# Sparse attention scores two heads at a time, block 0 with two products for three; the first weights by ScalarE's queue

## Chip, cores and metric

The kernel runs on one core of a Trainium2 chip. The metric is the device time of one execution in microseconds; a figure for a kernel is the median of its runs.

## What is computed

A decoder trunk of two layers on 512 tokens of width 2048, all in 32-bit floats. Layer one is sparse attention: an indexer picks 128 keys for each query, and 16 heads with 4 shared key/value heads attend to them. Layer two is stick-breaking attention. Each layer ends with a residual, a layer norm and a gated embedding. The part that the change touches most:

```python
proj = x @ w_in
q, k, v, gate, iq, ik, iw = jnp.split(proj, SPLITS_A, axis=-1)
...
# per block of 128 queries: n_sel = 128 keys, chosen by the indexer's scores
logits = jnp.einsum('bqngd,bqknd->bqngk', qg, ksel) * (HEAD_DIM ** -0.5)
logits = jnp.where(valid, logits, -jnp.inf)
wts = jax.nn.softmax(logits, axis=-1)
o = jnp.einsum('bqngk,bqknd->bqngd', wts, vsel)
...
return (o * jax.nn.silu(gate)) @ w_o
```

## The kernel before

Every product of 32-bit operands is done as three products of split operands. `split` writes the rounded part (`wh`, `xh`, `qh`, ...) with ScalarE and the rest (`wl`, `xl`, `ql`, ...) with VectorE; `mm3` (lines 136 to 138) multiplies high by high, low by high and high by low into one PSUM bank.

Weights come in tiles `raw` of 128x2x512, three in turn, issued by SP (`next_raw`, line 201 for the first pieces, 203 for the rest). `weight_parts` has three pairs `wh`, `wl` in turn. TensorE works in the order of the program text (`manual_schedule`); the order of VectorE, ScalarE and GpSimd is made by the framework's scheduler when the kernel is built, and each of these engines then works strictly in that order.

The start: VectorE writes a zero tile by a memset and a copy, TensorE runs six products of zeros (`spun`, line 158), and `first_items` splits the first pieces of x and of the weights of the indexer's queries (`iq`) and the keys (`k`).

The sparse attention runs over four groups g of four heads. `attend(g, Q)` is a generator: `scores(i)` for the query blocks i = 0 to 3 (block i has 128 (i + 1) keys), and `apply(i)`, which transposes the softmax tile (`pt`), splits it (`ph` by ScalarE, `pl` by VectorE) and multiplies by the values (`o`). Each head's score is an `mm3` into a bank `s`; VectorE adds the mask `am[i]` and takes the maximum in one custom instruction (reduction), a small step scales the maximum, ScalarE does exp with the sum, VectorE takes the reciprocal and scales. Score and transpose banks come from `spare`, which gives three banks in turn.

`interleave` puts steps of the gate projection (`gemm_w`, tiles `g`; one step is one `mm3`, 512 wide) between the yields of `attend`: first `lead` steps, then an even share of `n_fill` over `n_main` yields, and the rest at the end. `merge` takes in turn one step of `scores(i + 1)` and one of `apply(i)`. The place of the yields so sets how much other work TensorE has between one head's score and the next.

```python
yield from scores(0)
for i in range(4):
    following = scores(i + 1) if i < 3 else iter(())
    if i == 0:
        for _ in range(2):
            next(following)
            yield
    yield from merge(following, apply(i))
```

Of the kernel before, what the change touches and what calls it, by code (L numbers as in the profile page):

```python
# [10 lines left out]
F32 = mybir.dt.float32  # L11
F32R = mybir.dt.float32r
I32 = mybir.dt.int32
AF = mybir.ActivationFunctionType
ALU = mybir.AluOpType
# [3 lines left out]
T = 512  # L19
H = T // 2  # L20
# [36 lines left out]
def interleave(main, n_main, fill, n_fill, lead=0):  # L57

    steps(fill, lead)
    done = 0  # L60
    for i, _ in enumerate(main, 1):
        steps(fill, n_fill * i // n_main - done)
        done = n_fill * i // n_main
    run(fill)
# [13 lines left out]
def trunk_kernel(  # L78
# [56 lines left out]
    def mm3(out, a, b, start, stop):  # L135
        pe.matmul(out, a[0], b[0], start=start, stop=False)  # L136
        pe.matmul(out, a[0], b[1], start=False, stop=False)  # L137
        pe.matmul(out, a[1], b[0], start=False, stop=stop)  # L138
# [11 lines left out]
    def fblock(n):  # L150
        return F[n // 4][:, n % 4]

    zeros = XL[15][:, :128]
    dve.memset(fblock(0)[:, :128], 0.0)
    dve.tensor_copy(zeros, fblock(0)[:, :128])
    spun = bank(7, "spun")
    for _ in range(6):
        pe.matmul(spun.rearrange("p (a n) -> p a n", a=4), zeros, zeros.unsqueeze(1).broadcast_to([128, 4, 128]), start=True, stop=True)

    def plain(kb):  # L160
        return XH[kb], XL[kb]
# [17 lines left out]
    def next_raw():  # L179
        while sent[0] < len(units) and len(raws) < 3:  # L180
            raw = top.tile([128, 2, 512], F32, name="raw", tag="raw", bufs=3)
            unit = units[sent[0]]
            if len(unit) == 1:
                _, k, n = unit[0].shape
            else:
                k, n = 2, unit[-1]
            raw = raw.rearrange("p a n -> p (a n)")[:, : k * n].rearrange("p (k n) -> p k n", k=k)
            if len(unit) == 1:
                nc.sync.dma_start(raw, unit[0])
            else:  # L190
                src, a, b, c0, n = unit
                rows = src.rearrange("(k p) n -> p k n", p=128)
                step = b - a
                if sent[0] < 2:

                    for i, cut in enumerate(((0, H if sent[0] else NSEL, T), (0, T))):
                        for lo, hi in zip(cut, cut[1:]):
                            halves.append((raw[:, i, lo:hi], rows[:, a + i * step, c0 + lo : c0 + hi]))
                    if len(halves) == 6:
                        for n in (1, 3, 4, 2, 5, 0):  # L200
                            nc.sync.dma_start(*halves[n])
                else:
                    nc.sync.dma_start(raw, rows[:, a : b + 1 : step, c0 : c0 + n])
            raws.append(raw)
            sent[0] += 1
        return raws.popleft()
# [43 lines left out]
    def first_items():  # L250

        for k2 in range(NK // 2):
            x = next_raw()
            for n in (2 * k2, 2 * k2 + 1) if k2 else ():

                was, pinned[0] = pinned[0], k2 > 1
                split(*plain(n), x[:, n % 2])
                pinned[0] = was
            if k2 == 2:
                tc.keep_in_program_order(nc.sync.dma_start(rc, rope_c))  # L260
            if k2 in (2, 3):
                half = slice(64 * (k2 - 2), 64 * (k2 - 1))
                tc.keep_in_program_order(nc.sync.dma_start(posi[half], pos.broadcast_to([64, T])))
            if k2 == NK // 2 - 1:
                tc.keep_in_program_order(nc.sync.dma_start(lnc, ln_c))
            for c in range(2):
                raw = next_raw()
                if k2 == 0 and c:
                    split(*(part[:, :NSEL] for part in plain(0)), x[:, 0, :NSEL])
                for a in range(2):  # L270
                    wh, wl = weight_parts()
                    if k2 == c == 0:
                        cuts = ((NSEL, T), (0, H), (H, T)) if a == 0 else ((0, T),) * 2
                        for n, (lo, hi) in enumerate(cuts):
                            parts, src = (plain(a), x) if n == 0 else ((wh, wl), raw)
                            hp, lp = (part[:, lo:hi] for part in parts)
                            if n == 0:
                                dve.tensor_copy(hp, src[:, a, lo:hi])
                            else:
                                act.activation(hp, src[:, a, lo:hi], AF.Copy)  # L280
                            dve.tensor_tensor(lp, src[:, a, lo:hi], hp.bitcast(F32), ALU.subtract)
                    else:
                        split(wh, wl, raw[:, a])
                    yield wh, wl
# [4 lines left out]
    def gemm_w(items, get, banks, n=512, order=range(NK)):  # L289

        for i, kb in enumerate(order):
            wh, wl = next(items)
            x = get(kb)
            for j, out in enumerate(banks):
                a, b = j * 128, min(n, (j + 1) * 128)
                mm3(out[: b - a], (wh[:, a:b], wl[:, a:b]), x, i == 0, i == len(order) - 1)
                yield
# [442 lines left out]
    pi_.close()  # L740
    pkv_ = ExitStack()
    pkv = pkv_.enter_context(ss(name="pkv", bufs=1, side="right"))
    K = [tuple(pkv.tile([128, T], F32R, name=f"k{s}{g}") for s in "hl") for g in range(4)]
    V = [tuple(pkv.tile([128, 512], F32R, name=f"v{s}{t}") for s in "hl") for t in range(4)]

    def split_queries(g):
# [69 lines left out]
    def attend(g, Q):  # L816
        d = slice(g * 128, (g + 1) * 128)
        P = {}

        def scores(i):  # L820
            w = 128 * (i + 1)
            s = slice(i * 128, w)
            sm = pb.tile([128, 4, 4], F32, name="sm", tag="sm", bufs=2)
            P[i] = pb.tile([128, 4, 384 + 128 * (i % 2)], F32, name="p", tag=f"p{i % 2}")
            for h in range(4):
                ps = spare("s")
                mm3(ps[:, :w], [q[:, s] for q in Q[h]], [k[:, :w] for k in K[g]], True, True)
                p = P[i][:, h, :w]
                mx, nm, rs, ri = (sm[:, h, j : j + 1] for j in range(4))
                dve.tensor_tensor_reduce(p, ps[:, :w], am[i], 1.0, GONE, ALU.add, ALU.max, mx)  # L830
                dve.tensor_scalar(nm, mx, -HSCALE, None, ALU.mult)
                act.activation(p, p, AF.Exp, bias=nm, scale=HSCALE, accum_out=rs)
                dve.reciprocal(ri, rs)
                dve.tensor_scalar(p, p, ri, None, ALU.mult)
                yield

        def apply(i):
            po = bank(7, "o")
            ready = []

            def values(kb, parts):
                mm3(po, [v[:, d] for v in V[kb]], parts, kb == 0, kb == i)

            for kb in range(i + 1):
                pt = spare("pt")
                for h in range(4):
                    pe.transpose(pt[:, h * 128 : (h + 1) * 128], P[i][:, h, kb * 128 : (kb + 1) * 128], ident)
                parts = tuple(pb.tile([128, 512], F32R, name=f"p{x}", tag=f"p{x}", bufs=2) for x in "hl")
                split(*parts, pt)
                yield  # L850
                if ready:
                    values(*ready.pop())
                    yield
                ready.append((kb, parts))
            values(*ready.pop())
            act.activation(F[g][:, :, i * 128 : (i + 1) * 128], po.rearrange("p (h q) -> p h q", h=4), AF.Copy)
            yield

        yield from scores(0)
        for i in range(4):  # L860
            following = scores(i + 1) if i < 3 else iter(())
            if i == 0:
                for _ in range(2):
                    next(following)
                    yield
            yield from merge(following, apply(i))

    for g in range(4):
        banks = mm_banks("g")
        interleave(attend(g, Q), 36, gemm_w(items, plain, banks), 50 - 6 * (g == 0), lead=8 + 6 * (g == 0))  # L870
        if g < 3:
            Q = split_queries(g + 1)
        for h in range(4):
            sg = pb.tile([128, T], F32, name="sg", tag="sg", bufs=3)
            act.activation(sg, banks[h], AF.Silu)
            dve.tensor_tensor(F[g][:, h], F[g][:, h], sg, ALU.mult)
# [513 lines left out]
```

## Time and profile before

| | |
|---|---|
| median of 3 runs | 1872.39 us |
| lowest, highest | 1872.07, 1872.66 us |
| profiled execution | 1871.96 us |
| its span | 1870.2 us |
| TensorE busy | 1863.4 us (100%) |
| VectorE, ScalarE busy | 1196.2 (64%), 940.9 us (50%) |
| first scores of g = 0, 1, 2, 3 start at | 371.97, 431.11, 494.40, 557.66 us |
| in 372 to 608 us: VectorE, ScalarE busy | 147.44, 127.64 of 236.00 us |

The table's engine times are the sum of what each engine was busy with; busy shares say little by themselves where an engine waits in one stage and is pressed in another. PE is TensorE, DVE VectorE, ACT ScalarE; a line number is one of the kernel's, and line 111 is the helper through which all VectorE and ScalarE instructions go. A row of the timeline gives start, duration, engine, line, operation, output and inputs, shape, and in brackets the idle time of the engine before it and what ended that.

### The profile page before, as it was taken

The numbers are of one execution on the slowest core, as the hardware profiler recorded it, in microseconds if no ns is written. First come the engines' busy times: TensorE is split into PE (matmuls) and PEld (weight loads), VectorE is DVE, ScalarE is ACT, GpSimd is POOL, SyncE is SP. The second block draws the span as 40 slices with busy tenths as digits, with TensorE's granted clock in tenths as the row PEclk, the third lists the DMA queues.
The fourth block names the chain that finished last, engine by engine and source line by source line (L and its number), as shares of the span: only waits on it lengthen the run. The fifth ranks groups of instructions, "written<-read, shape, count | busy, mean of one in ns | idle before, by whom it ended". The sixth has DMA issues, their size and how long they took to land.

```text
span 1870.2 us, 24902 instructions
## 1 busy us (share of the span) xinstructions
PE 1863.4 (100%) x9229; PEld 1586.1 (85%) x9229; DVE 1196.2 (64%) x2326; ACT 940.9 (50%) x1712; POOL 26.8 (1%) x46
## 2 busy tenths in 40 slices
PE   9999999999999999999999999999999999999998
PEld 8898888888888888888888999988888888888887
DVE  5668678566556444675467788877656645567534
ACT  3546333355554432474245444478877743347422
POOL 0000000000000000000000000000100000000000
PEclk9999999999999999999999999999999999999999
DMA  6442333322222532333334333323222253243333
GB/s 197 127 121 61 102 90 102 91 67 68 68 69 59 162 117 79 124 101 102 124 124 124 102 102 102 108 85 90 59 68 69 64 183 100 74 130 94 120 102 113
DMA packets 111178, 189.21 MB, mean 101 GB/s; under 512 B 8528, under 2 KB 29008, under 8 KB 111056
## 3 DMA queue, kind: packets, MB, share of 16 engines
q1 hardware_dynamic: 111056, 187.62, 33.1%
q8 instruction: 72, 1.18, 0.3%
q14 instruction: 50, 0.41, 0.1%
HBM read 179.21 MB, written 8.39 MB: 100 GB/s over the span
## 4 chain that ended last, share of the span: by engine, by line
PE 99%; ACT 0%; DVE 0%; issue 0%; ACTq 0%
PE g L136 12%; PE g L138 12%; PE g L137 12%; PE o L137 7%; PE o L138 7%; PE o L136 7%; PE m L136 4%; PE m L138 4%; PE m L137 4%; PE q L137 3%; PE q L136 3%; PE q L138 3%; PE k L137 2%; PE k L138 2%; PE k L136 2%; PE z L1272 2%
## 5 line engine op out<-in xcount | busy, mean ns | idle before, releaser
L111 ACT ACTIVATE wh<-raw 128x512 fp32r<-128x512 f32 (+3 forms) x685 | 397.9, 582 | 702.0 <-PE g L137 234.1
L111 DVE TENSOR_TENSOR wl<-raw,wh 128x512 fp32r<-128x512 f32 (+3 forms) x685 | 430.9, 630 | 473.7 <-ACT wh L111 458.3
L136 PE MATMUL g<-xh,wh 128*128 128x512 f32 x1024 | 403.7, 394 | 0.1
L138 PE MATMUL g<-xh,wl 128*128 128x512 f32 x1024 | 399.4, 390 | 0.0
L137 PE MATMUL g<-xl,wh 128*128 128x512 f32 x1024 | 399.4, 390 | 0.0
L138 PEld LDWEIGHTS g<-xh,wl 128*128 128x128 f32 x1024 | 192.2, 188 | 40.8
L136 PEld LDWEIGHTS g<-xh,wh 128*128 128x128 f32 x1024 | 192.4, 188 | 38.3 <-ACT wk L111 0.8
L137 PEld LDWEIGHTS g<-xl,wh 128*128 128x128 f32 x1024 | 192.5, 188 | 37.0
L138 PE MATMUL o<-xh,wl 128*128 128x512 f32 x512 | 199.3, 389 | 0.0
L137 PE MATMUL o<-xl,wh 128*128 128x512 f32 x512 | 199.2, 389 | 0.0
L136 PE MATMUL o<-xh,wh 128*128 128x512 f32 x512 | 199.2, 389 | 0.0
L138 PEld LDWEIGHTS o<-xh,wl 128*128 128x128 f32 x512 | 96.1, 188 | 20.2 <-DVE wl L111 0.3
L137 PEld LDWEIGHTS o<-xl,wh 128*128 128x128 f32 x512 | 96.1, 188 | 20.1
L136 PEld LDWEIGHTS o<-xh,wh 128*128 128x128 f32 x512 | 96.1, 188 | 19.9
L136 PE MATMUL q<-xh,wh 128*128 128x512 f32 x256 | 99.6, 389 | 0.0
L137 PE MATMUL q<-xl,wh 128*128 128x512 f32 x256 | 99.6, 389 | 0.0
L138 PE MATMUL q<-xh,wl 128*128 128x512 f32 x256 | 99.6, 389 | 0.0
L111 ACT ACTIVATE sh<-st 128x512 fp32r<-128x512 f32 x80 | 49.7, 624 | 44.4 <-DVE st L111 44.3
L111 DVE TENSOR_TENSOR sl<-st,sh 128x512 fp32r<-128x512 f32 x80 | 55.2, 691 | 13.9 <-ACT sh L111 13.9
L111 DVE TENSOR_TENSOR xl<-f,xh 128x512 fp32r<-128x512 f32 x80 | 54.3, 686 | 12.6 <-ACT f L111 12.3
L111 ACT ACTIVATE wk<-z 128x512 f32<-128x512 f32 x80 | 47.2, 590 | 23.8 <-PE z L138 16.3
L136 PEld LDWEIGHTS q<-xh,wh 128*128 128x128 f32 x256 | 48.0, 188 | 10.1
(289 smaller groups left out, 3340.1 us busy)
## 6 DMA issues: line engine op xcount, KB each, us to landing
raw<-w_in_a SPq DMA_DIRECT2D x95, 512.0 KB, 3.7
raw<-w_in_b SPq DMA_DIRECT2D x64, 512.0 KB, 3.8
raw<-w_ple_gate SPq DMA_DIRECT2D x52, 512.0 KB, 3.7
raw<-w_o_a SPq DMA_DIRECT2D x24, 512.0 KB, 3.8
raw<-w_o_b SPq DMA_DIRECT2D x24, 512.0 KB, 3.7
raw<-w_kv_b SPq DMA_DIRECT2D x16, 512.0 KB, 3.7
raw<-w_ple_gate SPq DMA_DIRECT2D x24, 256.0 KB, 2.9
f<-xT SPq DMA_DIRECT2D x4, 1024.0 KB, 6.5
```

Source lines behind the costliest of these rows:

```text
L111: ins = method(*args, **kw)
L136: pe.matmul(out, a[0], b[0], start=start, stop=False)
L137: pe.matmul(out, a[0], b[1], start=False, stop=False)
L138: pe.matmul(out, a[1], b[0], start=False, stop=stop)
L1272: pe.matmul(z, m, p, start=False, stop=n == len(terms), skip_group_check=True)
```

## The change

The keys of a group are now one tile with the high and low parts side by side. For block 0 (128 keys) one product multiplies the high queries by both parts, 256 columns into the two halves of the bank, and a second one adds low queries by high keys onto the first half; a new VectorE instruction adds the mask to the second half, and the reduction takes that in place of the mask. For blocks 0 to 2, `scores` yields after every second head; block 3 yields after each. `attend` has 30 yields in place of 36, and one step of `scores(1)`, which is two heads, goes ahead of the merge in place of two steps of one head.

At the start the zero tile is one memset, the sixth warm-up product is half as wide, the first piece of weights is issued by ScalarE in place of SP, and its first half is split in two pieces of 128 columns, with the order of ScalarE and VectorE fixed for these.

```diff
-    dve.memset(fblock(0)[:, :128], 0.0)
-    dve.tensor_copy(zeros, fblock(0)[:, :128])
+    dve.memset(zeros.bitcast(F32), 0.0)
     spun = bank(7, "spun")
-    for _ in range(6):
-        pe.matmul(spun.rearrange("p (a n) -> p a n", a=4), zeros, zeros.unsqueeze(1).broadcast_to([128, 4, 128]), start=True, stop=True)
+    for n in (4, 4, 4, 4, 4, 2):
+        out = spun.rearrange("p (a n) -> p a n", a=4)[:, :n]
+        pe.matmul(out, zeros, zeros.unsqueeze(1).broadcast_to([128, n, 128]), start=True, stop=True)
...
                     if len(halves) == 6:
-                        for n in (1, 3, 4, 2, 5, 0):
+                        nc.scalar.dma_start(*halves[3])
+                        for n in (1, 4, 2, 5, 0):
                             nc.sync.dma_start(*halves[n])
...
                     if k2 == c == 0:
-                        cuts = ((NSEL, T), (0, H), (H, T)) if a == 0 else ((0, T),) * 2
+                        pinned[0] = a == 0
+                        cuts = ((NSEL, T), (0, 128), (128, H), (H, T)) if a == 0 else ((0, T),) * 2
...
+                        pinned[0] = False
...
-    K = [tuple(pkv.tile([128, T], F32R, name=f"k{s}{g}") for s in "hl") for g in range(4)]
+    KT = [pkv.tile([128, 2, T], F32R, name=f"k{g}") for g in range(4)]
+    K = [(kt[:, 0], kt[:, 1]) for kt in KT]
...
             for h in range(4):
                 ps = spare("s")
-                mm3(ps[:, :w], [q[:, s] for q in Q[h]], [k[:, :w] for k in K[g]], True, True)
                 p = P[i][:, h, :w]
                 mx, nm, rs, ri = (sm[:, h, j : j + 1] for j in range(4))
-                dve.tensor_tensor_reduce(p, ps[:, :w], am[i], 1.0, GONE, ALU.add, ALU.max, mx)
+                mask = am[i]
+                if i:
+                    mm3(ps[:, :w], [q[:, s] for q in Q[h]], [k[:, :w] for k in K[g]], True, True)
+                else:
+                    qh, ql = (q[:, s] for q in Q[h])
+                    two = ps[:, : 2 * w].rearrange("p (a k) -> p a k", a=2)
+                    pe.matmul(two, qh, KT[g][:, :, :w], start=True, stop=True)
+                    pe.matmul(ps[:, :w], ql, K[g][0][:, :w], start=False, stop=True, skip_group_check=True)
+                    mask = pb.tile([128, 128], F32, name="s1", tag="s1", bufs=2)
+                    dve.tensor_tensor(mask, two[:, 1], am[i], ALU.add)
+                dve.tensor_tensor_reduce(p, ps[:, :w], mask, 1.0, GONE, ALU.add, ALU.max, mx)
                 dve.tensor_scalar(nm, mx, -HSCALE, None, ALU.mult)
                 act.activation(p, p, AF.Exp, bias=nm, scale=HSCALE, accum_out=rs)
                 dve.reciprocal(ri, rs)
                 dve.tensor_scalar(p, p, ri, None, ALU.mult)
-                yield
+                if i == 3 or h % 2:
+                    yield
...
             if i == 0:
-                for _ in range(2):
-                    next(following)
-                    yield
+                next(following)
+                yield
             yield from merge(following, apply(i))
...
-        interleave(attend(g, Q), 36, gemm_w(items, plain, banks), 50 - 6 * (g == 0), lead=8 + 6 * (g == 0))
+        interleave(attend(g, Q), 30, gemm_w(items, plain, banks), 50 - 6 * (g == 0), lead=8 + 6 * (g == 0))
```

## The prediction

> **What bounds the kernel now.** I read the page first, then the waits of TensorE, then the timeline around the edited places.
>
> ```profile
> span 1870.2 us, 24902 instructions
> PE 1863.4 (100%) x9229; PEld 1586.1 (85%) x9229; DVE 1196.2 (64%) x2326; ACT 940.9 (50%) x1712; POOL 26.8 (1%) x46
> PE 99%; ACT 0%; DVE 0%; issue 0%; ACTq 0%
> PE spun L158 <- DVE xl L111: 1.4, 1, 1.4
> PE z L1272 <- DVE sl L111: 0.2, 1, 0.2
> ```
>
> TensorE is busy for all of the span, the chain that ended last is 99% TensorE, and the last two lines (waiter, releaser, us, times, longest) say that it waits for nobody after its start. So only two things move the end: TensorE getting fewer or shorter instructions, and TensorE being made to wait where it does not wait now. The order in which the build puts the instructions is the same before and after except in the first microseconds and in the four attention groups (372 to 608 us); nothing else has to be priced.
>
> **Part 1, fewer score products: a gain.** The timeline of TensorE at the first score of g = 1 and at a 256-wide one (start, duration, instruction):
>
> ```profile
> 430.65 0.39 PE L137 MATMUL g<-xl,wh 128*128 128x512 f32 x1
> 430.88 0.39 PE L138 MATMUL g<-xh,wl 128*128 128x512 f32 x1
> 431.11 0.22 PE L136 MATMUL s<-kh,qh 128*128 128x128 f32 x1
> 431.28 0.27 PE L138 MATMUL s<-kh,ql 128*128 128x128 f32 x1
> 431.67 0.40 PE L137 MATMUL g<-xl,wh 128*128 128x512 f32 x1
> 376.08 0.28 PE L136 MATMUL s<-kh,qh 128*128 128x256 f32 x1
> 376.19 0.28 PE L137 MATMUL s<-kl,qh 128*128 128x256 f32 x1
> 379.92 0.60 PE L847 MATMUL pt<-ident,p 128*128 128x128 f32 x4
> 380.59 0.39 PE L137 MATMUL g<-xl,wh 128*128 128x512 f32 x1
> ```
>
> Matmuls overlap, so their price is the distance of their starts. A 512-wide one takes a slot of 0.23, a gate step of three 0.68 to 0.69. From 431.11 to 431.67 lie three 128-wide products and one 512-wide: 0.56 - 0.23 = 0.33, 0.11 each. A 256-wide one takes 0.115 as well, so a 128-wide slot is not set by its columns. The changed pair of heads is 256, 128, 256, 128 wide: 2 x 0.115 + 2 x 0.11 = 0.45 in place of 0.66. Eight pairs (two in each of four groups) give 8 x 0.21 = **-1.7 us**. If a 128-wide slot behind a 256-wide one came down to half of 0.115, it would be 8 x 0.31 = -2.5; if the pair saved only one slot of 0.11, -0.9. I take -1.7, the rows of the same shapes.
>
> The Trainium skill ("TensorE: Matmul & The Clock Gate", section "Back-to-back issue gap") gives about 81 ns a matmul for a stream of 128-wide ones with their weight loads; the 0.11 of this trace is more, so by that figure, an estimate, the saving would be 8 x 0.09 = -0.7 us. The trace decides.
>
> **Part 2, the start.** The first rows:
>
> ```profile
> 0.80 0.38 SPq L201 DMA_DIRECT2D raw<-xT  x1
> 1.25 0.89 SPq L201 DMA_DIRECT2D raw<-w_in_a  x2
> 3.32 0.36 DVE L111 CAST xh<-raw 128x384 fp32r<-128x384 f32 x1 [2.00 <-DMA raw<-xT]
> 3.67 0.42 ACT L111 ACTIVATE wh<-raw 128x256 fp32r<-128x256 f32 x1 [1.58 <-DMA raw<-w_in_a]
> 3.71 0.56 DVE L111 TENSOR_TENSOR xl<-raw,xh 128x384 fp32r<-128x384 f32 x1
> 4.62 0.52 PE L137 MATMUL iq<-xl,wh 128*128 128x384 f32 x1
> 6.22 0.52 PE L136 MATMUL iq<-xh,wh 128*128 128x384 f32 x1
> 6.54 0.42 PE L137 MATMUL iq<-xl,wh 128*128 128x384 f32 x1
> 6.97 0.34 PE L136 MATMUL iq<-xh,wh 128*128 128x384 f32 x1
> 7.15 0.35 PE L137 MATMUL iq<-xl,wh 128*128 128x384 f32 x1
> ```
>
> The first weights are issued 0.45 behind x on SP; ScalarE's queue sends them at once, so wh comes up to 0.45 earlier and in a first piece of half the size. But xh is ready at 3.68 and xl at 4.27 whatever the weights do, and the second product needs xl: it moves from 4.62 to about 4.3. SP's later pieces move up by one issue. The table load of ScalarE goes behind the issue, 0.4 later, and ends well ahead of 3.3. The warm-up loses half a product and one VectorE instruction, beside the same DMA wait. I take **-0.3 us**, bounds -0.5 and +1.6: until 6.5 us the starts of the iq products lie 0.32 apart, later 0.17, and if the shorter warm-up put that step off by some 3 us, about half of that would be lost.
>
> **Part 3, two heads at a time: VectorE falls behind.** `attend` now yields 30 times for 36, and four heads of block 1 come ahead of the first transposes where three did. In the build's order for g = 1, between the first score and the first product of values (o) there were 12 gate steps, now 8 (one, two, two, one, then the transposes pt, then two). With pairs of 0.45 and 0.70, gate steps of 0.68 and pt at 380.59 - 379.92 - 0.23 = 0.44, TensorE gets there in 0.90 + 1.40 + 0.44 + 8 x 0.68 = 8.2, and o's second product, which reads pl, is due at **8.4 us** after the first score. Before, it started at 442.84, 11.7 after 431.11. VectorE has to make pl in that time:
>
> ```profile
> 372.60:382.79 10.19, 10.19 (x59) 8.77 (x57) 7.74 (x41) 7.05 (x19) 0.00 (x0) 1.00 0.32 92
> 431.59:441.61 10.02, 10.02 (x56) 8.56 (x56) 7.77 (x38) 6.71 (x19) 0.00 (x0) 1.00 0.30 97
> 558.14:568.20 10.06, 10.06 (x56) 8.62 (x56) 8.20 (x39) 7.25 (x20) 0.00 (x0) 1.00 0.29 94
> 431.59 0.29 DVE L111 CUSTOM_DVE_ANT_0 p<-s,am 128x128 f32<-128x128 f32 x1 [1.87 <-PE s L138]
> 431.81 0.69 DVE L111 TENSOR_TENSOR wl<-raw,wh 128x512 fp32r<-128x512 f32 x1
> 432.41 0.15 DVE L111 TENSOR_SCALAR sm<-sm 128x1 f32<-128x1 f32 x1
> 441.00 0.69 DVE L111 TENSOR_TENSOR pl<-pt,ph 128x512 fp32r<-128x512 f32 x1 [0.64 <-ACT ph L111]
> 441.61 0.15 DVE L111 RECIPROCAL sm<-sm 128x1 f32<-128x1 f32 x1
> 442.12 0.42 DVE L111 CUSTOM_DVE_ANT_0 p<-s,am 128x256 f32<-128x256 f32 x1
> 442.84 0.39 PE L137 MATMUL o<-pl,vh 128*128 128x512 f32 x1
> ```
>
> The first three rows are stretches from the first reduction to the end of pl in g = 0, 1 and 3 (length, then busy time of TensorE, weight loads, VectorE, ScalarE). In g = 1 VectorE was busy 7.8 of 10.0. The change adds four adds of mask and second half at 0.22 (the spacing of the 128x128 reduction, 431.59 to 431.81, the nearest row that reads a score bank), and the last two heads of block 1: VectorE's order puts pl behind all four, so a reciprocal and scaling (0.51, 441.61 to 442.12) for each and a reduction with its small steps (0.42 and these, 0.55) come ahead of it. One wl of 0.60 (431.81 to 432.41) drops out. 7.8 + 0.9 + 1.6 - 0.6 = 9.7, begun 0.4 after the first score (the second product starts at 0.115, and VectorE read 0.31 after a last product's start, 431.28 to 431.59): pl cannot end before 10.1. Queued ahead of it on ScalarE, ph stands behind all four exps. Due 8.4, ready 10.1: **1.7 us of waiting** in g = 1, and in g = 2, whose order is the same. Part of it falls earlier: the fourth head takes the first head's score bank again (three are in turn), and its reduction now stands behind two adds and a wl, so TensorE waits there some 0.5 first.
>
> g = 0: 7 gate steps, due at 7.75. Only one head's reciprocal, scaling and small step are new ahead of pl (0.64): 7.74 + 0.9 - 0.6 + 0.64 = 8.7, but there ScalarE's table load waits for the first maximum:
>
> ```profile
> 373.16 1.28 ACT L111 ACT_TABLE_LOAD   x1 [1.95 <-DVE sm L111]
> 374.98 0.16 DVE L111 RECIPROCAL sm<-sm 128x1 f32<-128x1 f32 x1 [1.21 <-ACT p L111]
> ```
>
> VectorE idled 1.21 behind it and will again, about 1.1. 0.4 + 8.7 + 1.1 = 10.2: **2.4 us**. g = 3: the build puts pl ahead of the last two scalings: 8.2 + 0.9 - 0.6 + 0.55 = 9.05, plus 0.4 is 9.45 against 8.4; **0.9**, as the order there leaves a little less. In block 2 the same happens once more in small: from the second pair to the second o TensorE needs 2 + 1 + 2 gate steps, pt and one o, 3.40 + 0.44 + 0.69 + 0.23 = 4.8 us.
>
> ```profile
> 447.18 0.69 DVE L111 TENSOR_TENSOR pl<-pt,ph 128x512 fp32r<-128x512 f32 x1 [0.24 <-ACT ph L111]
> 447.79 0.55 DVE L111 CUSTOM_DVE_ANT_0 p<-s,am 128x384 f32<-128x384 f32 x1
> 448.26 0.69 DVE L111 TENSOR_TENSOR wl<-raw,wh 128x512 fp32r<-128x512 f32 x1
> 445.58 0.62 ACT L111 ACTIVATE p<-p,sm 128x384 f32<-128x384 f32 x1 [1.33 <-DVE sm L111]
> ```
>
> VectorE and ScalarE have in a row a pl (0.6), two reductions (0.6 each), a wl (0.6), small steps (0.2), two exps (0.7 each), a scaling (0.5) and pl (0.6): 5.1 to 5.2. **0.4** in each group. Block 3 keeps one head at a time with more gate steps between: nothing.
>
> Waits: 1.7 + 1.7 + 2.4 + 0.9 + 4 x 0.4 = **+8.3**. A wait of TensorE is lost for good, as it has no idle time later to make it up. The bounds: +5.5 if block 2 fits and each first wait is 0.3 less, +16 if VectorE again idles the 2 us of each stretch that it idled before.
>
> **The sum.** -1.7 - 0.3 + 8.3 = +6.3. The profiled execution took 1871.96 us, so 1878.3; the median of the runs is 0.43 above it: **1878.7 us**.
>
> **Rivals.** *It pays, slightly.* VectorE keeps pace: 1872.4 - 2.0 = 1870.4. For it: VectorE was only 77% busy in these stretches, and before no score ever waited. Against: the idle 2.2 us is less than 9.7 - 7.8 plus the 3.3 us by which TensorE is early. It decides from where the sum ahead of pl is under 8 us. 12%. *Half of it.* The waits come to 2 to 5.5 us because VectorE's pieces close up more than their spacings: 1872.4 to 1875.9. 16%. *ScalarE too.* Every ph waits behind exps that wait for VectorE, its old idle times return and block 3 starts late: waits of 13 to 16 us, 1884 to 1887. 10%. *The start.* The warm-up ends too early and the fast step of TensorE comes a turn later: +1.6 on any of these, not a case of its own. The Trainium skill ("Trainium Kernel Development and Optimization", section "Key Constraints") says that issuing DMAs from several engines only saves the issue time; the 0.45 between the two issues is all I count, and a larger gain at the start would be against it.
>
> **How the numbers follow.** About 0.2%, 3.7 us, is what a measurement of this kernel tells from no change. The forecast (waits of 5.5 to 13) has 62%, the rivals 12, 16 and 10. The range holds the forecast, the half and most of the upper case: 1871.5 to 1886. Slower by over 0.2% means above 1876.1: the forecast and the upper case, 0.72. Faster by over 0.2% would need more than every gain above together: 0.03. Between: 0.25.
>
> **What would show it.** In the changed profile TensorE should have waits in the attention that it has not now: o on pl and ph of block 0, longest in g = 0, s on VectorE's reduction, 8 us in all; the pairs of scores 0.45 long; the first iq product some 0.3 earlier; VectorE without gaps from the first add to pl. If those stretches show no waits of TensorE, part 3 is wrong; if the waits stand in block 3 or in the gate steps, the place is wrong.

## The result, and the profile after

The changed kernel takes 1876.31 us (median of 14 runs, 1875.63 to 1877.02), the kernel before 1872.07 in the same sessions: 4.24 us or 0.23% slower, ratio 1.0023 with a 95% interval of 1.0014 to 1.0031. The profiled execution, the one of 1877.02 us, is the longest of the 14. One of the 14 executions of the kernel before took 2657.22 us, all others 1871.56 to 1872.66, and the ratio leaves it out.

The page, and the waits of TensorE (waiter, releaser, us, times, longest), of the changed kernel:

```profile
span 1875.3 us, 24910 instructions
PE 1865.4 (99%) x9213; PEld 1586.7 (85%) x9213; DVE 1195.4 (64%) x2342; ACT 939.9 (50%) x1713; POOL 26.6 (1%) x46
PE s L840 <- DVE sm L111: 1.0, 3, 0.3
PE iq L136 <- ACT wh L111: 0.7, 1, 0.7
PE o L136 <- ACT ph L111: 0.7, 1, 0.7
PE o L137 <- DVE pl L111: 0.7, 3, 0.2
```

Four waits are new: one at the start, three in the attention. The list counts a wait only where TensorE shows as idle; as the ends of matmuls are modelled, part of each wait hides in a long matmul. So I also take the time from a group's first score to the last product of its first o and subtract the slots (the usual distances of starts, 0.23 for a product 512 wide, 0.12 for 256, 0.11 for 128) of what lies between. What is left is time that TensorE lost on the way.

The start, by the timeline:

```profile
3.98 0.36 DVE L111 CAST xh<-raw 128x384 fp32r<-128x384 f32 x1 [2.91 <-DMA raw<-xT]
4.20 0.82 ACT L111 ACTIVATE wh<-raw 128x128 fp32r<-128x128 f32 x3 [1.68 <-DMA raw<-w_in_a]
4.57 0.69 PE L136 MATMUL iq<-xh,wh 128*128 128x384 f32 x1 [0.73 <-ACT wh L111]
9.95 0.52 PE L137 MATMUL iq<-xl,wh 128*128 128x384 f32 x1
10.27 0.46 PE L138 MATMUL iq<-xh,wl 128*128 128x384 f32 x1
10.57 0.34 PE L136 MATMUL iq<-xh,wh 128*128 128x384 f32 x1
10.74 0.34 PE L137 MATMUL iq<-xl,wh 128*128 128x384 f32 x1
```

x is split 0.66 later than before (3.98, not 3.32) and the weights 0.53 later (4.20, not 3.67), although the weights were issued earlier. TensorE idles 0.73 between warm-up and first product, and the spacing of the iq products stays at 0.32 until 10.57, where before it was 0.17 to 0.18 from 6.80 on:

```profile
6.80 0.34 PE L138 MATMUL iq<-xh,wl 128*128 128x384 f32 x1
```

The first score of g = 0 comes at 373.90, before at 371.97: 1.9 of this execution's 5.1 us are the start.

Group 1 of the attention, TensorE first, then VectorE and ScalarE, and the stretch from the first add to the end of pl (length, then busy time of TensorE, weight loads, VectorE, ScalarE):

```profile
434.43 0.28 PE L840 MATMUL s<-k,qh 128*128 128x256 f32 x1
435.12 0.40 PE L137 MATMUL g<-xl,wh 128*128 128x512 f32 x1
436.28 0.36 PE L840 MATMUL s<-k,qh 128*128 128x256 f32 x1 [0.34 <-DVE sm L111]
440.41 0.28 PE L136 MATMUL s<-k,qh 128*128 128x256 f32 x1
444.29 0.50 PE L137 MATMUL o<-pl,vh 128*128 128x512 f32 x1 [0.23 <-DVE pl L111]
435.24 0.68 DVE L111 TENSOR_TENSOR wl<-raw,wh 128x512 fp32r<-128x512 f32 x1
435.84 0.28 DVE L111 CUSTOM_DVE_ANT_0 p<-s,s 128x128 f32<-128x128 f32 x1
443.55 0.69 DVE L111 TENSOR_TENSOR pl<-pt,ph 128x512 fp32r<-128x512 f32 x1
442.44 0.49 ACT L111 ACTIVATE p<-p,sm 128x256 f32<-128x256 f32 x1
442.94 0.58 ACT L111 ACTIVATE ph<-pt 128x512 fp32r<-128x512 f32 x1
434.80:444.15 9.35, 8.83 (x47) 6.94 (x46) 8.46 (x47) 6.99 (x21) 0.00 (x0) 1.00 0.31 104
```

A pair of heads costs 435.12 - 434.43 - 0.23 = 0.46. The fourth head waits for its bank because the first head's reduction (435.84) stands behind a wl (435.24). The last head of block 1, whose score starts at 440.41, has its exp at 442.44; ph stands behind that exp, pl behind ph, and o's second product starts at 444.29, 9.9 after the group's first score, where 8.4 was due.

### The profile page after: what moved, and what is told of

Same layout as the page of the kernel before. It is cut to its first block, busy times and chain, and to the rows that moved or that the text cites. A ratio compares the mean times of both kernels' runs of the same rounds, so it can differ in the third digit from the quotient of the medians.

```text
span 1875.3 us, 24910 instructions
## 1 busy us (share of the span) xinstructions
PE 1865.4 (99%) x9213; PEld 1586.7 (85%) x9213; DVE 1195.4 (64%) x2342; ACT 939.9 (50%) x1713; POOL 26.6 (1%) x46
## 4 chain that ended last, share of the span: by engine, by line
PE 98%; DVE 1%; ACT 1%; issue 0%; DMA 0%; ACTq 0%
PE g L136 12%; PE g L137 12%; PE g L138 12%; PE o L137 7%; PE o L138 7%; PE o L136 7%; PE m L136 4%; PE m L138 4%; PE m L137 4%; PE q L137 3%; PE q L136 3%; PE q L138 3%; PE k L137 2%; PE k L138 2%; PE k L136 2%; PE z L1286 2%
```

## The experiments

All are built from the kernel before or the changed one and timed in five rounds beside the kernel before (medians 1871.76, 1872.02 and 1872.09 in the three sessions). The intervals of the ratios are 0.0008 to 0.0013 either way, 1.6 to 2.3 us, so single steps under 2 us rest on the spread of the runs and the traces.

**All attention edits, none of the start.** Edit: the second half of the diff (from `KT` on).

> Kernel before with all attention edits and none of the start. In the changed profile the first score of g = 0 starts 1.93 us late (371.97 to 373.90), and the chain behind the attention is 5.1 late, so the attention is worth +3.2. Theory (two separate costs that add): +3.2 us, 1875.2, with the first score at 372.0. Rival (the attention is late only because the start shifts the phase of the buffers): within 0.5 us of before.

Measured: 1875.21 us (1874.85 to 1875.59) against 1871.76, ratio 1.0018 (1.0009 to 1.0027): +3.45, as the theory had it, though the first score was at 372.44 in its profile.

**All start edits, attention as before.** Edit: the first half of the diff.

> Kernel before with all start edits and the attention as before. Theory (the start is a cost by itself: both first transfers land later and TensorE's fast step comes one turn later): +1 to +2 us. Rival (the start as predicted): -0.3 us. In the profile the 0.32 spacing of the iq products ends at about 10.4 us (theory) or 6.5 us (rival).

Measured: 1872.76 us (1871.82 to 1873.74) against 1871.76, ratio 1.0005 (0.9996 to 1.0014): +1.0 by the medians, not clear by its interval. The trace agrees with the theory: the spacing of 0.32 lasts to 10.05 and the first score is at 373.58. 3.45 + 1.0 make the 4.24 within 0.2.

**The two products and the add, one head at a time.**

```diff
-                if i == 3 or h % 2:
-                    yield
+                yield
...
-                next(following)
-                yield
+                for _ in range(2):
+                    next(following)
+                    yield
...
-        interleave(attend(g, Q), 30, ...
+        interleave(attend(g, Q), 36, ...
```

(against all attention edits)

> Kernel before with the two products and the new add, but one head at a time and 36 yields as before. Theory (waits come from the missing gate steps, not from the add): TensorE saves 16 x 0.1 = 1.6 us or a little less and waits nowhere new: -1.5 us. Rival (the adds are what VectorE has no room for): waits of 2 us and more, slower than before.

Measured: 1870.72 us, all of 11 runs between 1870.56 and 1870.83 against 1871.31 at the lowest before; ratio 0.9994 (0.9985 to 1.0003). It is the fastest kernel of this study, 1.0 better than the kernel before. The adds find room when the gate steps stay; TensorE's list has one new wait, 0.4 in g = 0.

**Two heads at a time, three products, no add.** Edit: only `if i == 3 or h % 2`, the single `next` and the 30.

> Kernel before with two heads at a time and 30 yields, but three products and no add. Theory: VectorE has 0.9 us less ahead of pl in each group than in the changed kernel, TensorE is 0.2 later per pair, so the waits of 4.9 us come down by about 3: +1 to +3 us. Rival (the adds make the waits): no waits, within 0.5 us of before.

Measured: 1875.34 us (1875.10 to 1876.31), ratio 1.0019 (1.001 to 1.0028): +3.6, above the theory's range, and far from the rival. So the batching makes the loss, the products give 1.0 back, and adds and batching together cost 0.9 more than apart.

**The shorter warm-up alone.** Edit: memset and the widths (4, 4, 4, 4, 4, 2).

> Kernel before with the shorter warm-up alone (one memset, five and a half products); the weights come by SP as before. Theory A (the fast step of TensorE comes late because it idles between the warm-up and the first product): the gap is here under 0.5 us, as the weights land as before at 3.7, and about half of the start's +1.0 us shows. Theory B (only the two queues cost, since x and the weights then land together and later): within 0.2 us of before.

**ScalarE's queue and the pieces of 128 alone.**

> Kernel before with the first weights by ScalarE's queue and the pieces of 128 columns in a fixed order, and the long warm-up. Theory B: x is split at about 4.0 and not 3.3, the weights at 4.2 and not 3.7, the first product some 0.5 late: +0.5 to +1 us. Theory A: the long warm-up keeps TensorE busy up to the first product, the fast step stays near 6.5 us: within 0.3 us of before.

**The changed kernel with eight full warm-up products.**

```diff
-    for n in (4, 4, 4, 4, 4, 2):
+    for n in (4,) * 8:
```

> The changed kernel with eight full warm-up products in place of five and a half, which covers the gap of 0.73 us ahead of the first product. Theory A: the fast step comes back to 6.5 to 7 us and the start's cost goes: 1.0 to 1.9 us faster than the changed kernel, 1875. Theory B: the transfers still land late: at most 0.3 faster.

Measured: 1872.20 (1871.80 to 1872.64), 1872.48 (1872.09 to 1872.70) and 1875.18 us (1875.04 to 1875.74) against 1872.02; ratios 1.0001 (0.9992 to 1.001), 1.0002 (0.9992 to 1.0011), 1.0017 (1.0009 to 1.0026). Alone neither edit loses more than 0.5; with the gap covered the changed kernel takes what the attention edits take alone. That fits A. The late landing of B is real too: x was split at 3.67 and 3.64 in the two with ScalarE's queue and at 3.16 in the other, but by itself it cost 0.5 at most. The start edits gain nothing in any form tried.

**Gate steps earlier.** Edit: 22 for 30 in `interleave`, in the changed kernel.

> The changed kernel with the gate steps spread over the first 22 yields in place of 30 (2.3 a yield in place of 1.7), the rest of the attention going without. Theory (VectorE is short of time between the first score and the first o): three to four gate steps more, 2.4 us, stand ahead of the first o, and its waits go; in the last yields TensorE has no gate steps left and waits for transposes instead, so the total may be no better. The waits on pl and ph of block 0 under 0.5 us in all, and about 1876 or more. Rival (waits come from the order of the engines, not from time): the waits at the first o stay at 1.4 us by TensorE's list.

Measured: 1876.88 us (1875.64 to 1877.42), ratio 1.0025 (1.0015 to 1.0034). The time lost up to the first o fell to 0.2 in g = 1, 2 and 3 (in the changed kernel 1.5, 1.5 and 0.7) and to 1.5 in g = 0 (2.0), by 3.6 in all. The kernel is no faster for it: the loss came back later. Weight loads of o waiting for pl, in 368 to 621 us:

```profile
PEld o L137 <- DVE pl L111: 4.8, 11, 0.7
PEld g L136 <- ACT sg L111: 1.2, 3, 0.4
```

In the changed kernel the first of these was 1.8 in 4 waits. Gate steps are what hides these chains, and there are only so many of them.

**Pairs in block 0 alone.** Edit: `if i or h % 2`, two `next`, 34 yields, on all attention edits.

> Kernel before with the two products, and two heads at a time in block 0 alone (34 yields, two steps of one head ahead of the merge); the start as before. Theory (the waits come from drawing the heads of block 1 together ahead of the first transposes): 10 gate steps for 8 stand ahead of the first o of g = 1 and one head's softmax less is ahead of pl, so the waits go but for a few tenths; the pairs of block 0 save 1.7 us: 1.0 to 1.6 us faster than before, at least as good as one head at a time (-1.0). Rival (any pair makes TensorE wait for its bank): +0.5 us or more.

Measured: 1872.55 us (1871.82 to 1872.87) against 1872.09, ratio 1.0002 (0.9993 to 1.0011). The theory missed: the waits at o went, but not the one for the bank.

```profile
PE s L837 <- DVE sm L111: 1.0, 3, 0.3
PE o L137 <- DVE sm L111: 0.2, 1, 0.2
```

**Pairs in blocks 0 and 1.** Edit: `if i > 1 or h % 2`, 32 yields, on all attention edits.

> All attention edits, but block 2 one head at a time (32 yields); the start as before. Theory (waits at the first o and at the fourth head's bank make all of it, block 2 fits): about as all attention edits, +3 to +3.5 us against before. Prediction on record (block 2 waits 0.4 in each group): 1.6 less, near +1.8.

Measured: 1877.86 us (1877.33 to 1879.10, 5 runs), ratio 1.0033 (1.002 to 1.0045): +5.8, worse than with block 2 in pairs too. Both expectations missed: with 32 yields one gate step fewer lies ahead of the first o, between pt and o, and TensorE waits for ph in each group.

```profile
PE o L136 <- ACT ph L111: 2.3, 4, 1.4
PE o L137 <- DVE pl L111: 0.9, 4, 0.2
```

**Without the add.**

```diff
-                    mask = pb.tile([128, 128], F32, name="s1", tag="s1", bufs=2)
-                    dve.tensor_tensor(mask, two[:, 1], am[i], ALU.add)
```

> All attention edits, the start as before, but the second half of block 0's bank is left out: no add, the reduction takes the mask as before. VectorE has 0.9 us less in each group. Theory (VectorE is short of time up to pl): the waits fall by about 0.9 in each group at most, 2 to 3 us in all: +0.5 to +1.5 us against before. Rival (the order of ph behind four exps alone): the wait for the bank goes (1 us), the rest stays: +2.5.

Measured: 1874.50 us (1873.99 to 1874.65), ratio 1.0013 (1.0004 to 1.0021): +2.4. It is the rival's number: the wait for the bank went, those at o stayed.

**Without reciprocal and scaling in blocks 0 and 1.** The exps of these blocks are then not divided by their sum.

```diff
-                dve.reciprocal(ri, rs)
-                dve.tensor_scalar(p, p, ri, None, ALU.mult)
+                if i > 1:
+                    dve.reciprocal(ri, rs)
+                    dve.tensor_scalar(p, p, ri, None, ALU.mult)
```

> All attention edits, the start as before, but reciprocal and scaling of blocks 0 and 1 are left out, 8 of each in a group, some 3 us of VectorE's time ahead of pl. Theory (VectorE's time): the waits at the first o go, that for the fourth head's bank (a wl and two adds ahead of the reduction) stays at 1 us by TensorE's list: 0 to -1 us against before. Rival (order: ph behind four exps): the waits for ph stay, +2 us and more.

Measured: 1874.08 us (1873.91 to 1874.51), ratio 1.0011 (1.0002 to 1.002): +2.0, again the rival's. Its timeline, and its stretch from the first add to pl in g = 1 (length, then busy time of TensorE, weight loads, VectorE, ScalarE):

```profile
432.00:441.05 9.05, 8.71 (x48) 7.04 (x47) 5.88 (x31) 6.93 (x21) 0.00 (x0) 1.00 0.34 108
437.39 0.28 PE L136 MATMUL s<-k,qh 128*128 128x256 f32 x1
438.87 0.51 ACT L111 ACTIVATE p<-p,sm 128x256 f32<-128x256 f32 x1 [0.53 <-DVE sm L111]
439.37 0.49 ACT L111 ACTIVATE p<-p,sm 128x256 f32<-128x256 f32 x1
439.86 0.57 ACT L111 ACTIVATE ph<-pt 128x512 fp32r<-128x512 f32 x1
440.47 0.69 DVE L111 TENSOR_TENSOR pl<-pt,ph 128x512 fp32r<-128x512 f32 x1 [1.52 <-ACT ph L111]
441.22 0.50 PE L137 MATMUL o<-pl,vh 128*128 128x512 f32 x1 [0.17 <-DVE pl L111]
```

VectorE is busy 5.9 of 9.05 and sits idle 1.52 ahead of pl, and TensorE still waits. What is late is a chain: the last pair of scores at 437.39, its reductions, its two exps, ph behind them, pl, o. To cover it TensorE has only the pair (0.70), three gate steps (2.1), pt (0.44) and o's first product (0.23), 3.4 in all; the chain takes 3.8, 437.39 to 441.22.

The time lost between a group's first score and the last product of its first o, as defined above, over the kernels (gate steps ahead of that o in g = 0 and in the others; then us in g = 0, 1, 2, 3):

| kernel | gate steps | g = 0 | 1 | 2 | 3 |
|---|---|---|---|---|---|
| before | 11, 12 | 0.1 | 0.1 | 0.1 | 0.1 |
| changed | 7, 8 | 2.0 | 1.5 | 1.5 | 0.7 |
| one head at a time, two products | 11, 12 | 0.8 | 0.1 | 0.1 | 0.1 |
| pairs, three products | 7, 8 | 1.3 | 1.0 | 1.0 | 1.0 |
| without the add | 7, 8 | 1.6 | 1.0 | 1.0 | 1.1 |
| without scaling | 7, 8 | 1.2 | 1.1 | 1.1 | 1.1 |
| pairs in block 0 | 9, 10 | 0.7 | 0.7 | 0.7 | 0.7 |
| pairs in blocks 0 and 1 | 6, 7 | 2.6 | 1.7 | 1.7 | 1.8 |
| gate steps earlier | 10, 11 | 1.5 | 0.2 | 0.2 | 0.2 |

Without the adds the wait is 1.0 or 1.1 wherever 8 gate steps lie ahead. With them come some 0.5 at the bank (g = 1 to 3). In g = 1 of the changed kernel that leaves 0.9 at o, without scaling 0.5. So VectorE's lateness is worth some 0.4 in such a group, and the chain the other 0.5.

Group 3 of the changed kernel shows the chain by another way. It has the same 8 gate steps and the same adds, but there the build put ph ahead of the two exps of the last pair, and pl ahead of their scalings:

```profile
570.47 0.60 ACT L111 ACTIVATE ph<-pt 128x512 fp32r<-128x512 f32 x1 [1.08 <-PE pt L862]
570.97 0.50 ACT L111 ACTIVATE p<-p,sm 128x256 f32<-128x256 f32 x1
571.88 0.47 PE L137 MATMUL o<-pl,vh 128*128 128x512 f32 x1
```

Of its 0.7 the bank has some 0.5 and the wait at o only 0.1, where g = 1 with ph behind the exps loses 0.9 at o. In the run without the add the build put ph behind the exps in g = 3 too, and 1.0 is lost at o. No run sets this order in the other groups, so what it would bring there is not shown.

## Why the prediction was right, and where it was not

**What bounds it**: right. Nothing outside the start and the attention moved: from the first score of g = 3 to the end of the span both kernels take 1312.5 us. The 5.1 us between the two profiled executions are 1.9 at the start and 1.4, 0.9 and 0.9 between the first scores of g = 0, 1, 2 and 3.

**Part 1**: the pair costs 0.46, forecast 0.45, so eight give 1.6, forecast 1.7. One head at a time, the edit gave 1.0.

**Part 2**: wrong in its sign, -0.3 against +1.0 by the medians. The failed step is "wh comes up to 0.45 earlier ... it moves from 4.62 to about 4.3": x and weights, sent at once by two queues, both landed later, and the late step to the spacing of 0.17, kept as a bound of +1.6, is what the profiles with both start edits show. "Beside the same DMA wait" was wrong too: the shorter warm-up ended ahead of it.

**Part 3**, the waits at the first o and the bank: forecast 2.4, 1.7, 1.7, 0.9, together 6.7; found 2.0, 1.5, 1.5, 0.7, together 5.7 by the trace. Place, order of the groups and the wait of 0.5 for the fourth head's bank were right, and in g = 0 VectorE idled 1.08 behind the table load, as forecast (1.1). The reason was half right. "VectorE falls behind" was priced as a sum of VectorE's work, 9.7 in g = 1 without a gap; it was 8.5 with gaps of 0.9, and pl ended 9.7 after the first score, not 10.1. The run without scaling took some 3 us of that work out and left the wait at o at 0.5 of 0.9. The rest is the chain named only in passing, "ph stands behind all four exps", with too few gate steps between the last pair and o. That the two prices came out alike is no proof of the first. In g = 3 the 0.9 came near the 0.7 by luck: it was priced as VectorE's lateness at o, and nearly all of it is the wait for the bank.

**Block 2**, 4 x 0.4 = 1.6: nothing. The 1.5 us lost at the first o of g = 1 are 1.6 at both o that lie among the scores of block 2, and in the kernel before the same sum grows by as much. Both lengths were priced about right, but not where they start:

```profile
450.09 0.68 DVE L111 TENSOR_TENSOR pl<-pt,ph 128x512 fp32r<-128x512 f32 x1
450.88 0.39 PE L136 MATMUL g<-xh,wh 128*128 128x512 f32 x1
454.30 0.68 DVE L111 TENSOR_TENSOR pl<-pt,ph 128x512 fp32r<-128x512 f32 x1
455.72 0.39 PE L137 MATMUL o<-pl,vh 128*128 128x512 f32 x1
```

The chain from one pl to the end of the next took 4.8 us (450.09 to 454.90), forecast 5.1 to 5.2. TensorE's 4.8 us run from the end of the second pair, 450.88, to 455.72. The step that failed is setting the two starts equal: the chain begins 0.8 earlier, beside the second pair, and pl is ready 0.8 before o reads it.

**The sum**: -1.6 + 1.0 + 5.3 (5.7 less the 0.4 that the same measure gives before) = +4.7 for the 4.24 found, where +6.3 was forecast: 1876.3 in place of 1878.7, 2.4 us less. Waits were put too high by 3.0, the start too low by 1.3. By its waits, 5.3, this is the upper end of the rival "half of it" (2 to 5.5), not the forecast's own case (5.5 to 13). That the total still came out over the 0.2% is luck: the start, forecast as a gain, brought it there. The times of the rival "ScalarE too" were added up wrong: 1872.4 - 2.0 with 13 to 16 us of waits is 1883.4 to 1886.4, not 1884 to 1887.

## What to carry to other kernels

Where a saturated engine works in a fixed order, filler between a producer and the first reader of its chain is a resource: count it in time, from the last producer and not only from the first, before drawing producers together. A sum of another engine's work finds where it falls short, but not the chain through two in-order queues; lay out that chain too, and test by taking work out of one engine. Look also at where the build puts the chain's links in these queues: in g = 3 the same work in another order waited 0.1 at o in place of 0.9. Parts of a change that save little by themselves should be run by themselves: two products for three gave 1.0 us where the whole change lost 4.2.

## What had not been expected of the hardware

Two first transfers sent at once by two queues: x was split at 3.64 to 3.98 us in the five kernels that use ScalarE's queue and at 3.15 to 3.35 in the nine that send it ahead of the weights on SP, with its own issue unchanged at 0.80. The Trainium skill ("Trainium Kernel Development and Optimization", section "Key Constraints") says that queues of several engines share the same DMA engines and only save issue time; these runs add that the transfer that was first before can lose by it. SP's later pieces went out earlier as well in these five kernels (the second one of x at 1.71, not 2.18), and no run takes that apart from the second queue.

The step of the iq spacing from 0.32 to 0.17 lay between 4.5 and 7.7 us in the eleven kernels whose first product came without an idle time of 0.5 or more, and at 10.25, 10.43 and 10.57 in the three that idled 0.52 to 0.73, all with the short warm-up and ScalarE's queue. Each figure is from one execution, and among the eight kernels that start as before the step already lies anywhere from 4.7 to 7.7. The granted clock of the profile shows 1.00 throughout, so only the spacing tells it. The Trainium skill ("TensorE: Matmul & The Clock Gate", section "What's actually happening") has a free-running window of about 3.4 us that must be busy; a spread of 3 us between kernels with the same start and a jump of some 3 us with a gap would fit a window of that length. The 500 ns either way that the same section gives for the place of the step are less than the spread measured here. Whether the gap alone does it was not separated from the phase of that window.
